# The first layer's leading products from x itself, with the tokens' factors applied to the outputs

## The chip, the cores and the metric

The kernel runs on one core of one Trainium2 chip. The metric is device time in microseconds (us) for one execution. TensorE (PE) does matrix products into PSUM banks, VectorE (DVE), ScalarE (ACT) and GpSimd (POOL) do elementwise work, SyncE (SP) issues most loads and stores. The engines run at the same time, each in its own fixed order, and wait for one another through semaphores.

## What is computed

Two layers of an encoder over 512 tokens of width 1024. Each layer begins with a normalisation and one wide projection; its output feeds a neighbourhood attention (A), a dilated attention (B) and an attention into 256 memory tokens (M), which are gated, merged and projected; then comes a gated MLP. What matters for this change:

```python
def rms_norm(x, g):
    xf = x.astype(jnp.float32)
    y = xf * lax.rsqrt(jnp.mean(xf * xf, axis=-1, keepdims=True) + RMS_EPS)
    return (y * g.astype(jnp.float32)).astype(x.dtype)

def reference(x, mem, mem_norm_g, g_pre_mix, w_in, ...):
    mem_n = rms_norm(mem, mem_norm_g)
    for l in range(DEPTH):
        h = rms_norm(x, g_pre_mix[l])
        proj = h @ w_in[l]
        q_a, k_a, v_a, q_b, k_b, v_b, q_m, gate_pre = jnp.split(proj, splits, axis=-1)
...
        o_m = memory_attention(q_m, mem_n, w_mem_kv[l])
```

The factor `rsqrt(mean(x*x) + eps)` is one number for each token. In the product `h @ w_in` it can stand in front of the sum over the 1024 channels: the gain `g` cannot, since it differs from channel to channel.

## The kernel before

**Layout.** Everything is held transposed: channels on the 128 partitions, tokens along the free dimension. x is eight tiles of 128 channels by 512 tokens (k = 0 to 7). Tokens are handled in two halves of 256 where a normalisation is waited for.

**Products in three parts.** Each float32 operand is split into a high part (a rounded copy by ACT, `split`, L220) and a low part (the difference, by DVE or POOL). `mm3` (L246) makes high x high, high x low and low x high. A weight tile is loaded by SP into a raw buffer (`wraw`, three of them), then split by `weights` (L224). With `slot` given, high and low parts go into tiles of 512 columns from a pool: two ACT casts and two differences for each weight tile.

**The leading products.** In front of each normalised stage, six output tiles are computed together in six PSUM banks (`group_banks`, L427, `run_group`, L430): in layer 0 the output tiles `FIRST` = 0, 3, 6, 1, 4, 7, that is q, k and v of two pairs of heads of A. They run as three pairs (0, 1, 2 in the text), for half 0 and then for half 1; for each k a pair takes six matmuls of 256 columns. Their inputs come from `pre_norm_job` (L347): `first_squares` (L782) squares x on ACT and adds on DVE; `rstd_job` (L323) sums over the partitions with products against a column of 1/1024, takes Sqrt on ACT and the reciprocal on DVE, multiplies the identity with the factors (two diagonal matrices, DVE), and one float32 product with a matrix of ones spreads the factors over all partitions in a PSUM bank; `normed` (L342) makes x * g * factor on DVE, the high part on ACT and the low part on DVE, for each k.

**The order.** `Woven` (L46) fixes PE's order: it keeps a clock of the PE work issued so far (`clk`), jobs with due times on that clock are put between the matmuls by `tick`, and `need` runs jobs until a flag is given. The orders of the other engines follow from a planner at build time that goes by the order of issue and by when it takes the inputs to be ready. The start of the kernel (L792 to L805) issues: x's first half, the constants (`ident`, `vec`, which holds the gains, and `mg` on POOL's queue), the squares, two weight tiles, x's second half, the normalisation of half 0, then that of half 1 four units later, the other four weight tiles, the tables, and the memory tokens' normalisation (`mem_norm_job`, L380, whose loads are on ACT's queue).

**After the leading products** the keys and values of the memory come (`mem_kv`, L408, called at L813), then the evacuations of the six banks (`a_q`, `a_k`, `a_v`), a third triple of projections (`proj`, L442), and the projections of B, between which the heads of A run as jobs.

**Pools.** `mp` holds 32 tiles of 512 columns (`big`), `hp` 16 more (`htile`) for the normalised tiles and some weights. `ytile` is a pool of 8.

Of the kernel before, what the change touches and what calls it, by code (L numbers as in the profile page):

```python
# [7 lines left out]
F32 = mybir.dt.float32  # L8
# [24 lines left out]
V_N = 232  # L33
# [86 lines left out]
def tile_hybrid_encoder(ctx, tc, xT, memT, memg, vecs, rpb, w_in, w_kv, w_bra, w_brb, w_brm,  # L120
# [6 lines left out]
    mp = ctx.enter_context(tc.tile_pool(name="mp", bufs=32))  # L127
    hp = ctx.enter_context(tc.tile_pool(name="hp", bufs=16))
# [17 lines left out]

    def htile(dt=F32R, shape=(128, 512)):
        return hp.tile(list(shape), dt, tag="h", name=nm("h"))
# [41 lines left out]
    def load_x(half):  # L190
        for k in range(0, KD, 2):
            nc.sync.dma_start(out=xs[k // 4][:, k % 4:k % 4 + 2, half], in_=xT[:, k:k + 2, half])

    load_x(HALVES[0])
# [5 lines left out]
    ones = const.tile([128, 128], F32, name="ones")  # L200
    nc.gpsimd.memset(ones, 1.0)
# [4 lines left out]
    vec = const.tile([128, depth, V_N], F32, name="vec")  # L206
    nc.gpsimd.dma_start(out=vec, in_=vecs)
# [16 lines left out]
    def weights(src, K, C, slot=None, eng=None, after=None):  # L224

        raw = wp.tile([128, K, C], F32, tag="wraw", name=nm("wraw"))
        nc.sync.dma_start(out=raw, in_=src)
# [95 lines left out]
    def rstd_job(accs, n, box):  # L323
# [11 lines left out]
        diag = small("h32", 4, (128, n))  # L335
        for b in range(nb):
            V.tensor_scalar_mul(diag[:, 128 * b:128 * b + 128], ident, rs[:, b:b + 1])
        yield 1.2
        mm(pr, ones, diag, True, True, n * 4 / 2400.0)
        box.append(pr)  # L340

    def normed(src, g, rs, hi, lo, eng=None):  # L342
        h32 = small("h32", 4)
        V.scalar_tensor_tensor(out=h32, in0=src, scalar=g, in1=rs, op0=ALU.mult, op1=ALU.mult)
        split(h32, hi, lo, eng)

# [29 lines left out]
    def h_tiles():  # L376
        return [(htile(), htile()) for _ in range(KD)]


    def mem_norm_job(l, hm, slot):  # L380
# [5 lines left out]
        acc = small("h32", 4)  # L386
# [43 lines left out]
    def run_group(grp, hs, half, flag, cols=None):  # L430
# [4 lines left out]
        for i in range(0, len(ws), 2):  # L435
            for k in range(n):
                rhs = [t[:, half] for t in hs[k]]
# [365 lines left out]
    hm = []  # L803
    wv.spawn(mem_norm_job(0, hm, big), 6.0)
    km, vm = [], []  # L805
# [205 lines left out]
```

## Time and profile before

| | us |
|---|---|
| runs before, median of 3 | 1577.96 (1577.94 to 1579.77) |
| the profiled execution | 1579.04 |
| its span, first to last instruction | 1577.3 |
| busy in the span: PE | 1529.7 |
| busy in the span: DVE | 911.2 |
| busy in the span: ACT | 727.4 |
| busy in the span: POOL | 186.4 |

A row of the order of time reads: start, time to the end of the merged instructions, engine, line of the kernel, operation, output <- inputs, shapes, count, and in brackets the idle time in front and what ended it. A helper records most operations of ACT and DVE, so they all have its line (L114); matmuls have L244. In the groups by line the columns behind the bar are busy time in us and mean duration in ns, and behind the second bar the idle time just in front. Tiles go by the program's names without numbers: `h` and `m` are pool tiles, `mm`, `s`, `o` and `pt` PSUM banks, `wraw`, `whi`, `wlo` weight tiles, `y` work tiles.

### The profile page before, as it was taken

The numbers are of one execution on the slowest core, as the hardware profiler recorded it, in microseconds if no ns is written. First come the engines' busy times: TensorE is split into PE (matmuls) and PEld (weight loads), VectorE is DVE, ScalarE is ACT, GpSimd is POOL, SyncE is SP. The second block draws the span as 40 slices with busy tenths as digits, with TensorE's granted clock in tenths as the row PEclk, the third lists the DMA queues.
The fourth block names the chain that finished last, engine by engine and source line by source line (L and its number), as shares of the span: only waits on it lengthen the run. The fifth ranks groups of instructions, "written<-read, shape, count | busy, mean of one in ns | idle before, by whom it ended". The sixth has DMA issues, their size and how long they took to land.

```text
span 1577.3 us, 21375 instructions
## 1 busy us (share of the span) xinstructions
PE 1529.7 (97%) x8246; PEld 1316.4 (83%) x8246; DVE 911.2 (58%) x1654; ACT 727.4 (46%) x1289; POOL 186.4 (12%) x244
## 2 busy tenths in 40 slices
PE   6999999999999999999989999999999999999997
PEld 5988888889898888878888888888898888888887
DVE  6686566344866666542386856743457666664233
ACT  5465575334544444532345646733454544444231
POOL 4340000110400000010062300001121000000000
PEclk9999999999999999999999999999999999999998
DMA  7222213224213222333331221132431232223331
GB/s 241 87 78 67 66 56 100 88 94 134 81 42 106 93 95 96 115 97 100 115 113 49 86 69 56 51 120 74 140 101 48 69 105 95 94 96 96 99 103 62
DMA packets 46614, 144.96 MB, mean 92 GB/s; under 512 B 5232, under 2 KB 11376, under 8 KB 46512
## 3 DMA queue, kind: packets, MB, share of 16 engines
q1 hardware_dynamic: 44656, 139.61, 27.7%
q10 hardware_dynamic: 1152, 2.10, 0.5%
q0 software_dynamic: 704, 1.88, 0.4%
q8 instruction: 65, 1.06, 0.3%
q14 instruction: 37, 0.30, 0.1%
HBM read 141.47 MB, written 2.10 MB: 91 GB/s over the span
## 4 chain that ended last, share of the span: by engine, by line
PE 88%; DVE 8%; ACT 2%; issue 1%; DMA 1%; SPq 0%; ACTq 0%
PE mm L244 73%; PE s L244 6%; PE o L244 3%; PE pt L244 2%; DVE h L114 2%; PE pt L255 2%; DVE y L114 2%; DVE x L114 1%; DVE m L114 1%; DVE wlo L114 1%; ACT whi L114 1%; DVE acc L114 1%; DVE ka L114 0%; ACT y L114 0%; DMA m<-in_memT_dram 0%
## 5 line engine op out<-in xcount | busy, mean ns | idle before, releaser
L244 PE MATMUL mm<-h,whi 128*128 128x512 f32 x2432 | 755.7, 392 | 0.0
L244 PEld LDWEIGHTS mm<-h,whi 128*128 128x128 f32 x2432 | 449.6, 188 | 88.7
L114 DVE TENSOR_TENSOR wlo<-wraw,whi 128x1024 fp32r<-128x1024 f32 (+1 forms) x203 | 246.9, 1218 | 394.9 <-ACT whi L114 394.8
L244 PE MATMUL mm<-h,wlo 128*128 128x512 f32 x1216 | 473.9, 390 | 0.0
L114 ACT CAST whi<-wraw 128x1024 fp32r<-128x1024 f32 (+1 forms) x203 | 210.3, 1038 | 296.5 <-PE mm L244 295.7
L244 PEld LDWEIGHTS mm<-h,wlo 128*128 128x128 f32 x1216 | 228.2, 188 | 48.5
L244 PE MATMUL mm<-m,whi 128*128 128x512 f32 (+1 forms) x672 | 178.2, 354 | 1.6 <-DVE m L114 0.8
L244 PEld LDWEIGHTS mm<-m,whi 128*128 128x128 f32 x672 | 119.6, 192 | 19.0 <-PE mm L244 1.3
L114 DVE SCALAR_TENSOR_TENSOR y<-mm,vec,y 128x511 f32<-128x511 f32 x160 | 118.9, 746 | 8.5 <-ACT y L114 5.9
L244 PE MATMUL mm<-m,wlo 128*128 128x512 f32 (+1 forms) x336 | 118.3, 352 | 0.7 <-DVE wlo L114 0.7
L114 ACT ACTIVATE y<-mm,vec 128x512 f32<-128x512 f32 (+1 forms) x163 | 113.6, 698 | 0.1
L244 PE MATMUL mm<-m,m 128*128 128x512 f32 (+1 forms) x432 | 88.6, 346 | 0.0
L222 POOL TENSOR_TENSOR m<-wraw,m 128x512 fp32r<-128x512 f32 x42 | 56.3, 1355 | 238.5 <-ACT m L114 234.2
L728 POOL TENSOR_TENSOR m<-m,y 128x512 f32<-128x512 f32 x28 | 36.1, 1289 | 405.7 <-DVE y L114 405.7
L244 PEld LDWEIGHTS mm<-m,m 128*128 128x128 f32 x432 | 67.6, 190 | 8.4
L244 PEld LDWEIGHTS mm<-m,wlo 128*128 128x128 f32 x336 | 64.4, 192 | 9.4 <-DVE wlo L114 1.1
L114 ACT ACTIVATE y<-y 128x512 f32<-128x512 f32 x44 | 27.8, 632 | 87.3 <-DVE y L114 87.3
L244 PE MATMUL mm<-h,m 128*128 128x256 f32 x456 | 63.6, 296 | 4.0 <-ACT h L114 1.6
L114 DVE TENSOR_TENSOR acc<-acc,sq 128x256 f32<-128x256 f32 (+1 forms) x86 | 44.6, 521 | 37.5 <-ACT sq L114 36.9
L114 ACT CAST m<-wraw 128x512 fp32r<-128x512 f32 (+1 forms) x98 | 56.1, 602 | 21.1 <-DMA wraw<-in_w_brb_dram 9.5
L244 PEld LDWEIGHTS mm<-h,m 128*128 128x128 f32 x456 | 59.2, 199 | 6.4 <-ACT h L114 2.8
L114 ACT CAST m<-pt 128x512 fp32r<-128x512 f32 (+1 forms) x72 | 38.2, 539 | 40.4 <-PE pt L255 32.0
(150 smaller groups left out, 1835.8 us busy)
## 6 DMA issues: line engine op xcount, KB each, us to landing
wraw<-in_w_in_dram SPq DMA_DIRECT2D x88, 512.0 KB, 3.3
wraw<-in_w_up_dram SPq DMA_DIRECT2D x88, 512.0 KB, 3.3
wraw<-in_w_down_dram SPq DMA_DIRECT2D x32, 512.0 KB, 3.5
wraw<-in_w_out_dram SPq DMA_DIRECT2D x16, 512.0 KB, 3.4
wraw<-in_w_down_dram SPq DMA_DIRECT2D x16, 384.0 KB, 3.1
wraw<-in_w_kv_dram SPq DMA_DIRECT2D x8, 512.0 KB, 3.6
wraw<-in_w_bra_dram SPq DMA_DIRECT2D x16, 192.0 KB, 2.3
x<-in_xT_dram SPq DMA_DIRECT2D x8, 256.0 KB, 7.2
```

What stands on the lines that cost most here:

```text
L114: return op(*args, **kw)
L222: last_lo[eng or V] = (eng or V).tensor_sub(lo, src, f32(hi)).ins
L244: wv.pe(nc.tensor.matmul(ps, a, b, start=first, stop=last), cost)
L255: wv.pe(nc.tensor.transpose(ps[:, 128 * i:128 * i + 128], s, ident), 0.11)
L728: (V if br == 2 and m >= 6 else G).tensor_add(acc[m], acc[m], gs)
```

## The change

Half 0 of the first layer's leading products no longer uses normalised tiles. `raw_split` makes the high and low part of x * g, without the token factors; the products run on these (`xg`) into columns 0 to 255 of the six banks. Half 1 runs on normalised tiles as before. A tile `R` holds the factors of half 0 (copied from PSUM) and 1.0 for half 1; after both halves every bank is multiplied by `R` into a work tile (`scaled`), and the evacuations read that tile. Half 0 is normalised all the same, later, since all other projections use it: `first_norm_job(1, R)` is due at 13 units, `first_norm_job(0, R)` at 22.

The loads of x's first half and of the first two weight tiles, cut into halves, alternate on SP's queue. The gains (`vec`) are loaded on ACT's queue ahead of everything. All weight tiles of this group have their low parts on DVE; two of them follow the split of x, then x's second half is issued, then the last two. The memory tokens' normalisation is spawned after the first pass of the products, and `mem_kv` runs after the third triple of projections.

In every `rstd_job` the diagonal matrices and the product with ones are replaced by two products of the identity with the factors' column, read 128 times by a zero step; the pause in front of them falls from 1.2 to 0.8 units. The pools `mp` and `hp` become one of 48; what used `htile` uses `big`.

```diff
-    mp = ctx.enter_context(tc.tile_pool(name="mp", bufs=32))
-    hp = ctx.enter_context(tc.tile_pool(name="hp", bufs=16))
+    mp = ctx.enter_context(tc.tile_pool(name="mp", bufs=48))
...
-    load_x(HALVES[0])
+    vec = const.tile([128, depth, V_N], F32, name="vec")
+    nc.scalar.dma_start(out=vec, in_=vecs)
...
+    def load_w(src, K, C, ks=None, raw=None):
+        if raw is None:
+            raw = wp.tile([128, K, C], F32, tag="wraw", name=nm("wraw"))
+        ks = ks or slice(0, K)
+        nc.sync.dma_start(out=raw[:, ks, :], in_=src[:, ks, :])
+        return raw
...
-        diag = small("h32", 4, (128, n))
+        yield 0.8
         for b in range(nb):
-            V.tensor_scalar_mul(diag[:, 128 * b:128 * b + 128], ident, rs[:, b:b + 1])
-        yield 1.2
-        mm(pr, ones, diag, True, True, n * 4 / 2400.0)
+            one = rs[:, b:b + 1]
+            spread = bass.AP(one.tensor, one.offset, [list(one.ap[0]), [0, 128]])
+            mm(pr[:, 128 * b:128 * b + 128], spread, ident, True, True, 0.22)
...
+    def raw_split(l, goff, k, src, hi, lo):
+
+        g = vec[:, l, goff + k:goff + k + 1]
+        ACT.activation(hi, src, AF.Copy, scale=g)
+        V.scalar_tensor_tensor(out=lo, in0=src, scalar=g, in1=f32(hi), op0=ALU.mult, op1=ALU.subtract)
...
+    def scaled(ps, R):
+        y = ytile()
+        V.tensor_mul(y, ps, R)
+        return y
...
-    hs = h_tiles()
-    wv.spawn(pre_norm_job(0, V_PRE, first_squares(HALVES[0]), hs, 0))
-    gw = group_weights([w_in[0, m] for m in FIRST[:2]], (V, G))
+    def first_norm_job(i, R):
+
+
+        half, box = HALVES[i], []
+        yield from rstd_job(first_squares(half), 256, box)
+        if i == 0:
+            ACT.copy(R[:, half], box[0])
+        for k in range(KD):
+            normed(x[k][:, half], vec[:, 0, V_PRE + k:V_PRE + k + 1], box[0], hs[k][0][:, half], hs[k][1][:, half])
+        crit[0] = last_copy[0]
+        yield 1.2
+        wv.give(f"h0.{V_PRE}.{i}")
+
+    hs, R = h_tiles(), rtile()
+    nc.gpsimd.memset(R[:, HALVES[1]], 1.0)
+    xg = [big(F32R, (128, 2, 256)) for _ in range(KD)]
+    xg = [(t[:, 0, :], t[:, 1, :]) for t in xg]
+    load_x(HALVES[0], (0,))
+    raws = [load_w(w_in[0, m], KD, 128, slice(0, 4)) for m in FIRST[:2]]
+    load_x(HALVES[0], (2,))
+    for m, raw in zip(FIRST, raws):
+        load_w(w_in[0, m], KD, 128, slice(4, 8), raw)
+    load_x(HALVES[0], (4, 6))
+    gw = []
+    for k in range(KD):
+        raw_split(0, V_PRE, k, x[k][:, HALVES[0]], *xg[k])
+        if k == 0:
+            gw += [weights(None, KD, 128, big, raw=raw) for raw in raws]
+    gw += group_weights([w_in[0, m] for m in FIRST[2:4]], (V, V))
     load_x(HALVES[1])
-    wv.need(f"h0.{V_PRE}.0")
-    with tc.issue_after(last_copy[0]):
-        sqs = first_squares(HALVES[1])
-    wv.spawn(pre_norm_job(0, V_PRE, sqs, hs, 1), SD1)
-    gw += group_weights([w_in[0, m] for m in FIRST[2:]], (V, G, V, G))
+    gw += group_weights([w_in[0, m] for m in FIRST[4:]], (V, V))
+    wv.spawn(first_norm_job(1, R), 13.0)
+    wv.spawn(first_norm_job(0, R), 22.0)
...
     for l in range(depth):
         pss = group_banks()
-        for i in range(2):
-            run_group((gw, pss), hs, HALVES[i], f"h{l}.{V_PRE}.{i}")
+        if l == 0:
+            run_group((gw, pss), xg, FULL, None, HALVES[0])
+            wv.spawn(mem_norm_job(0, hm, big), 6.0)
+            run_group((gw, pss), hs, HALVES[1], f"h0.{V_PRE}.1")
+            wv.need(f"h0.{V_PRE}.0")
+            pss = [scaled(ps, R) for ps in pss]
+        else:
+            for i in range(2):
+                run_group((gw, pss), hs, HALVES[i], f"h{l}.{V_PRE}.{i}")
         fence = crit[0]
-        if l == 0:
-            mem_kv(l, hm, km, vm)
...
+        if l == 0:
+            mem_kv(l, hm, km, vm)
```

More of the change, by code (lines that the diff above doesn't have):

```diff
@@ L222, in split, with weights @@
         last_lo[eng or V] = (eng or V).tensor_sub(lo, src, f32(hi)).ins
-    def weights(src, K, C, slot=None, eng=None, after=None):
-        raw = wp.tile([128, K, C], F32, tag="wraw", name=nm("wraw"))
-        nc.sync.dma_start(out=raw, in_=src)
+    def load_w(src, K, C, ks=None, raw=None):
[4 more added lines that the diff above has]
+        return raw
+    def weights(src, K, C, slot=None, eng=None, after=None, raw=None):
+        if raw is None:
+            raw = load_w(src, K, C)
         if slot is None:
@@ L376, in h_tiles @@
     def h_tiles():
[L377 removed]
+        return [(big(), big()) for _ in range(KD)]
     def mem_norm_job(l, hm, slot):
```

28 lines of the change are left out of this document (11 added, 17 removed).

## The prediction

> **What bounds the kernel now.** I read the busy times first, then the chain that ended last, then the busy time of stretches, and last the order of time of the first 60 us.
>
> ```profile
> span 1577.3 us, 21375 instructions
> PE 1529.7 (97%) x8246; PEld 1316.4 (83%) x8246; DVE 911.2 (58%) x1654; ACT 727.4 (46%) x1289; POOL 186.4 (12%) x244
> ...
> PE 88%; DVE 8%; ACT 2%; issue 1%; DMA 1%; SPq 0%; ACTq 0%
> ...
> 0.00:12.00 12.00, 1.84 (x8) 1.78 (x8) 2.46 (x6) 4.57 (x12) 5.98 (x35) 1.00 0.81 264
> 12.00:48.00 36.00, 31.19 (x220) 29.64 (x221) 30.44 (x64) 20.73 (x51) 15.09 (x16) 1.00 0.59 198
> 48.00:58.40 10.40, 10.40 (x89) 10.40 (x88) 7.30 (x19) 3.81 (x11) 1.73 (x3) 1.00 0.11 42
> 58.40:71.50 13.10, 12.19 (x100) 11.84 (x99) 7.17 (x10) 6.40 (x11) 7.35 (x13) 1.00 0.28 91
> 71.50:130.00 58.50, 57.16 (x311) 48.51 (x309) 48.45 (x128) 38.79 (x88) 19.56 (x25) 1.00 0.27 89
> 130.00:160.00 30.00, 29.96 (x154) 25.08 (x153) 14.58 (x31) 14.46 (x26) 1.08 (x2) 1.00 0.19 60
> ```
>
> TensorE (PE) is busy for 97% of the span, and the chain of waits runs through it for 88%, so only two things can shorten the kernel: PE work removed or PE gaps closed. The second part of the fence is busy time per stretch (start:end, length, then busy us of PE, PEld, DVE, ACT, POOL, the clock, the DMA share, GB/s). PE has nothing to do for 10 of the first 12 us. The profiled execution took 1579.04 us, its span 1577.3; the median of the three shown is 1577.96. I sum against 1579.04 and subtract the 1.1 us between it and the median at the end.
>
> ```profile
> 9.90 1.84 PE L244 MATMUL pt<-mean,y 128*128 128x1 f32 x8 [9.90 <-DVE y L114]
> 15.10 0.58 PE L244 MATMUL mm<-h,m 128*128 128x256 f32 x1 [1.01 <-ACT h L114]
> 16.65 7.65 PE L244 MATMUL mm<-h,m 128*128 128x256 f32 x41 [0.96 <-DVE h L114]
> 25.20 0.60 PE L244 MATMUL pt<-mean,y 128*128 128x1 f32 x4 [0.90 <-DVE y L114]
> ...
> 47.80 5.02 PE s L244 x42
> ...
> 58.42 0.40 PE L244 MATMUL mm<-m,whi 128*128 128x256 f32 x2
> ```
>
> In order of time: the first PE work is the sum of squares (9.90), the first leading product comes at 15.10, the last ends where the memory keys begin (58.42). The leading products are 6 banks x 2 halves x 8 x 3 = 288 matmuls of 256 columns. Run without a gap, 42 take 5.02 us in the chain of waits, 0.12 each: 288 need 34.6 us. From 0 to 58.42 PE thus loses some 20 us after the small norm products (1.84 and 0.60 among them, about 4 in all): about 15 before the first, the rest while 41 matmuls take 7.65 us because they follow the normalised tiles one by one. That stretch is what the change touches.
>
> **The change, part by part.** *The start.* Half 0 no longer waits for squares, means, Sqrt, reciprocal, diagonals and spread: it waits for a column of x, the gain vector and a weight half, then one ACT cast and one DVE instruction for each.
>
> ```profile
> 0.75 1.97 SPq L192 DMA_DIRECT2D x<-in_xT_dram  x4
> 2.77 0.94 SPq L227 DMA_DIRECT2D wraw<-in_w_in_dram  x2
> ...
> 0.00:10.00 10.00, 0.10 (x1) 0.13 (x1) 2.37 (x6) 4.35 (x10) 5.98 (x35) 1.00 0.75 241
> 10.00:20.00 10.00, 6.87 (x26) 5.79 (x27) 7.81 (x20) 5.86 (x14) 2.64 (x2) 1.00 0.88 296
> ...
> DMA to landing us min/median/max: 2.8/7.2/8.4
> DMA to landing us min/median/max: 4.8/5.8/6.6
> ...
> DMA to landing us min/median/max: 7.3/7.4/8.1
> ```
>
> First two issues on SyncE's queue, then the DMA rate of two stretches, then the landing times of x, of the memory tiles on ACT's queue, and of the first weight tiles. 241 GB/s are 2.4 MB by 10.0. In the new order x's first half (1.05 MB), two weight tiles (1.05) and the constants (0.3) are 2.4 MB, so the eighth column lands at 10 to 11 whatever the interleaving; the first lands at 0.75 + 2.8 = 3.5. The gain vector moves from POOL's queue to the head of ACT's; a load on that queue has landed after 4.8 to 6.6 us, an x load after 2.8: 3.6 to 7.4. Behind the cast that waits for it stand the weight casts in ACT's order, so PE waits for the vector too. POOL's queue only loses an issue: the identity comes no later.
>
> ```profile
> L114 DVE TENSOR_TENSOR h<-h,h 128x256 fp32r<-128x256 f32 x16 | 8.8, 565 | 1.1 <-ACT h L114 1.1
> L222 POOL TENSOR_TENSOR m<-wraw,m 128x512 fp32r<-128x512 f32 x6 | 8.0, 1356 | 17.0 <-ACT m L114 17.0
> L114 DVE SCALAR_TENSOR_TENSOR h<-x,vec,pt 128x256 f32<-128x256 f32 x16 | 7.1, 471 | 0.2 <-PE pt L244 0.2
> L114 ACT CAST m<-wraw 128x512 fp32r<-128x512 f32 x12 | 6.7, 615 | 0.0
> L114 ACT CAST h<-h 128x256 fp32r<-128x256 f32 x16 | 6.4, 402 | 4.0 <-DVE h L114 3.8
> L114 DVE TENSOR_TENSOR m<-wraw,m 128x512 fp32r<-128x512 f32 x6 | 3.9, 683 | 0.0
> ...
> L114 DVE TENSOR_TENSOR y<-y,y x6: 411/422/1536, 22.0 to 25.1; 128x256 f32<-128x256 f32 x6
> ...
> 92.15 0.69 DVE L114 TENSOR_TENSOR m<-pt,m 128x512 fp32r<-128x512 f32 x1 [0.85 <-ACT m L114]
> ```
>
> Durations (busy time over count): a 128x256 scalar-tensor-tensor 0.44 us, a 128x256 cast 0.40, a weight cast 0.56, a weight difference 0.65 on DVE and 1.36 on POOL; a 128x256 add 0.42 (the median), a 128x512 tensor-tensor from PSUM 0.69. The 128x256 differences average 0.55, but those beside no POOL work took 0.42, and after the change no weight difference runs on POOL in this stretch. The new scalar-tensor-tensor for x (cast, then 0.44) and the PSUM multiply have these rows as their nearest.
>
> PE could start between 5.5 (vector at 3.6) and 9.4 (vector at 7.4), the last 1.9 being an x cast, a weight cast, a weight difference and their hand-overs; I take 7.0. Pair 0 then follows the loads: last column at 10.5, two casts and differences and 6 matmuls, end at 13.0. Pair 1 needs the fourth weight tile, which waits for the first raw buffer and may go to the queue before or after x's second half (1.05 MB, 3.6 us at 290 GB/s): landed at 13.3 or 16.9, usable 1.2 later (0.56 + 0.65). I take 16.0; end 21.8. Pair 2's last tile is landed at 20.5 in both orders: 21.8 to 27.6, with one norm job's PE work inside (0.60 for the means in the 25.20 row, as much for the two spread products): 28.8. Half 1's first tile comes after that job's spread: 0.44 + 0.40 + 0.42, of which one k (0.72) is covered: 29.4. Its three pairs take 17.3, the first paced by DVE at 0.86 for 0.72 (+1.1), and half 0's own norm job adds 1.2: 49.0. **Lead: 58.4 - 49.0 = 9.4 us earlier.** Best case 7.0 + 34.6 + 2.4 = 44.0, so 14.4. Worst case: 2.1 more for a fourth tile usable at 18.1 and 2.9 for a wait of the same kind in front of the last tile: 54.0, so 4.4.
>
> *A cold array.* The first 15 matmuls are slower than the later ones in the same bank:
>
> ```profile
> L244 PE MATMUL mm<-h,m x15: 415/415/580, 16.6 to 19.8; 128*128 128x256 f32 x15
> ...
> L244 PE MATMUL mm<-h,m x27: 279/283/415, 19.8 to 24.0; 128*128 128x256 f32 x27
> ```
>
> 415 against 283 ns until 20 us, though the granted clock reads 1.00. Started at 7.0 at this cost, six matmuls take at most 6 x (0.12 + 0.13) = 1.5 us, so three ks pass before 11.5, when the last columns arrive anyway: I cost it at 0, and at 4.5 us if all of pair 0 stayed slow. The Trainium skill, "TensorE: Matmul & The Clock Gate", section "Part 1: The HAM clock gate", says that the array runs at half speed until it has been busy for about 3.4 us. The slow rows end 3.3 us after 16.65, which agrees. The rule speaks against a start on trickling data: an estimate by that page is half of 3.4, 1.7 us lost, and the sum would be 1571.3.
>
> *The norm job everywhere.* Two diagonal multiplies on DVE and a product with ones become two products of the factors' column spread by a zero step. 18 jobs have it; on PE it matters where PE waited for the diagonals:
>
> ```profile
> 412.88 0.67 PE L244 MATMUL pt<-h,ones 128*128 128x256 f32 x2 [1.47 <-DVE h L114]
> 787.61 0.67 PE L244 MATMUL pt<-h,ones 128*128 128x256 f32 x2 [1.27 <-DVE h L114]
> 812.65 0.67 PE L244 MATMUL pt<-h,ones 128*128 128x256 f32 x2 [3.04 <-DVE h L114]
> 1188.61 1.19 PE L244 MATMUL pt<-h,ones 128*128 128x256 f32 x2 [0.89 <-DVE h L114]
> 1567.70 0.48 DVE L114 TENSOR_SCALAR h<-ident,st 128x128 f32<-128x128 f32 x2
> 1568.34 0.99 PE L244 MATMUL pt<-h,ones 128*128 128x256 f32 x2 [1.16 <-DVE h L114]
> ```
>
> The chain loses 0.48 of DVE and about 0.15 of handover, 0.63 us. The yield falls from 1.2 to 0.8, so the product also stands 0.4 earlier in PE's order with less cover. Five waits then give 0.23 to 0.63 each: 1.2 to 3.2; I take 2.0, and 0 as the low end (the next wait, on the cast, ends last). The zero-step weight load is in no row; the nearest is the ones pair, 0.67: no gain or loss there, half a microsecond either way.
>
> *Multiplying the outputs.* A projection of the third triple, from the chain of waits:
>
> ```profile
> 85.53 5.46 PE mm L244 x24
> ```
>
> Six 0.69 multiplies, 4.1 us of DVE, four of them beside half 1's last products, the last two behind it. The next PE work, the third triple of projections, has a free third bank and needs half 0's normalised tiles, which DVE makes meanwhile (8 x 0.86 = 6.9). On DVE the evacuations and that triple's weight differences stand behind the multiplies, which themselves wait for ACT's copy of the factors, one of 0.4. This triple (3 x 5.46 = 16.4 us of PE) now covers the six evacuations that the 13.1 us of memory keys covered. I cost it at 0 on PE; without that cover it is the 1.4 us of the last two.
>
> *Memory keys later; DVE.* PE does the same 13 us of key work, so the move is free unless DVE cannot follow. DVE was busy 95.8 us up to 130 (the first five stretches). Added: three weight tiles taken from POOL, 6 x 0.65 = 3.9; x's differences 8 x 0.44 = 3.5; multiplies 4.1; removed three diagonal pairs, 1.4: 105.9. The same point should now come at 120.6 (130 - 9.4), with DVE idle for the first 6: 92% full. From 71.5 to 130 it was at 48.45 of 58.50, 83%, from 12 to 48 at 85%, neither at its limit. At 90% it needs 105.9/0.90 + 6 = 123.7. I take that, +3.1; bounds 0 (130 to 160 has DVE only half busy, and a lag there need not reach PE) and the gap at 83%, 133.6 - 120.6 = 13.0.
>
> *One pool of 48* in place of 32 and 16: the tiles are the same number, and in the first stretch 16 + 8 + 24 are exactly 48, so the memory tiles, four issues on ACT's queue, wait until the eight x tiles come free at about 29; they land some 6 us later, well ahead of the third triple. Later stages keep their order of requests: 0, up to 2 either way.
>
> Sum: -9.4 - 2.0 + 3.1 = -8.3: 1570.7 beside 1579.04, or **1569.6** on the median's footing.
>
> **The rivals.** (1) *All of the lead is kept:* loads arrive without gaps and DVE follows: 14.4 + 2 - 1.5 = 15 less, 1563. For it: the loads need only 20 of the 44 us. Against it: pair 1 waits for a tile that waits for a buffer. (2) *DVE becomes the bound behind the lead.* If it fills to 83% only, PE reaches the old 130 mark at 133.6: 3.6 later, less 2.0 elsewhere: 1579.5. (3) **Slower:** the same place at 80% or less: 105.9/0.80 + 6 = 138.4, 8.4 later, 2 back: 1584. It decides from about 82%, where the waits behind DVE stand in PE's fixed order (heads' transposes) and the other projections cannot pass them. For it: 58.40 to 71.50 and 71.50 to 130.00 already left PE idle for 0.9 and 1.3 us. Against it: less POOL work in the way of DVE's differences, and DVE's light stretch behind. (4) *The early start does not come:* the gain vector is last (7.4) and the fourth tile stands behind the second half of x and the tables: lead 4.4, norm jobs 2.0, given back 3.1: 1574.6, at the edge of what can be told apart, and counted there as no change.
>
> **How the numbers follow.** Forecast 0.58; rival 1 0.14; rival 2 0.12; rival 3 0.10; rival 4 0.06. 0.2% is 3.2 us, about what a measurement of this kernel can tell from no change: the bound lies at 1574.8 and 1581.2. Faster: forecast and rival 1, 0.72; within: rivals 2 and 4, 0.18; slower: 0.10. The range leaves out rival 3 and the better half of rival 1: 1562 to 1580.
>
> **What would show it.** The first leading product at 6 to 9 us instead of 15.10; the first projection with whi tiles (no key work before it) at 47 to 52; pair 1 starting when its second tile lands; DVE above 88% between 10 and 115 with PE waits on DVE below 5 us there; the listed norm waits each shorter by half a microsecond. The prediction is wrong if the start is later than 10, if PE waits more than 10 us behind DVE between 49 and 120, or if a stage after 160 changes by more than 3 us.

## The result, and the profile after

| | us |
|---|---|
| before, median of 4 runs | 1578.63 (1577.94 to 1579.77) |
| after, median of 4 runs | 1598.33 (1597.16 to 1599.57) |
| ratio | 1.0119, interval 1.0102 to 1.0136 |
| predicted | 1569.6, range 1562 to 1580 |

The change makes the kernel 20 us slower; it was forecast to be 9 us faster. Below are, of the kernel after, the busy times, the shares of the chain that ended last, and busy time by stretch in the same stretches and columns as in the prediction.

```profile
span 1597.8 us, 21397 instructions
PE 1537.3 (96%) x8282; PEld 1325.2 (83%) x8282; DVE 902.3 (56%) x1638; ACT 733.3 (46%) x1298; POOL 180.8 (11%) x237
...
PE 84%; DVE 8%; issue 4%; ACT 2%; DMA 1%; POOL 0%; SPq 0%; ACTq 0%; POOLq 0%; DVEq 0%
```

```profile
0.00:12.00 12.00, 3.59 (x10) 2.49 (x11) 4.21 (x9) 6.30 (x13) 5.73 (x34) 1.00 0.81 273
12.00:48.00 36.00, 35.41 (x279) 35.01 (x279) 23.42 (x59) 18.78 (x50) 0.00 (x0) 1.00 0.48 170
48.00:58.40 10.40, 3.93 (x29) 3.29 (x27) 10.27 (x21) 8.21 (x15) 4.11 (x6) 0.78 0.04 13
58.40:71.50 13.10, 8.10 (x29) 6.57 (x30) 6.54 (x7) 0.86 (x2) 9.07 (x10) 0.65 0.26 90
71.50:130.00 58.50, 52.37 (x310) 46.34 (x309) 47.54 (x123) 36.30 (x83) 21.71 (x31) 0.94 0.27 82
130.00:160.00 30.00, 30.00 (x169) 25.79 (x169) 21.32 (x53) 17.32 (x37) 3.52 (x7) 1.00 0.24 83
```

From 12 to 48 PE is fuller than before (35.4 of 36 us, against 31.2): the early start works. From 48 to 71.5 PE is busy for 12.0 of 23.5 us where it was busy for 22.6, and the granted clock reads 0.78 and 0.65 where it read 1.00. The DVE column names the stretch in front of it: 10.27 of 10.40 us. From 130 to 160 DVE is busy for 21.3 us where it was busy for 14.6, but PE is full there.

The order of time on PE, rows with a wait, and one row where the second pair of banks begins:

```profile
5.98 1.30 PE L244 MATMUL mm<-m,m 128*128 128x256 f32 x3 [5.98 <-ACT m L114]
9.50 1.60 PE L244 MATMUL mm<-m,m 128*128 128x256 f32 x4 [2.22 <-ACT m L114]
...
18.47 5.92 PE L244 MATMUL s<-m,m 128*128 128x256 f32 x48
...
31.77 0.38 PE L244 MATMUL mm<-m,m 128*128 128x256 f32 x1 [0.29 <-ACT m L114]
...
52.67 0.73 PE L244 MATMUL mm<-m,whi 128*128 128x512 f32 x2 [1.47 <-ACT whi L114]
63.40 0.79 PE L244 MATMUL mm<-m,wlo 128*128 128x512 f32 x1 [10.00 <-DVE wlo L114]
81.64 1.09 PE L255 MATMUL pt<-ident,sq 128*128 128x128 f32 x4 [4.22 <-DVE h L114]
104.22 0.44 PE L255 MATMUL s<-ident,m 128*128 128x128 f32 x2 [1.91 <-ACT m L114]
```

The lead ends at 51.2 (52.67 less the wait of 1.47), 7.2 us earlier than the 58.42 of before. Then the third triple of projections starts at once, and after its first two products it waits 10.0 us for the low part of its weights. What DVE does meanwhile:

```profile
53.45 0.68 DVE L114 TENSOR_TENSOR y<-pt,R 128x512 f32<-128x512 f32 x1
54.14 1.39 DVE L114 TENSOR_TENSOR m<-y,m 64x512 fp32r<-64x512 f32 x2
55.54 1.70 DVE L114 SCALAR_TENSOR_TENSOR ka<-y,ka 64x512 fp32r<-64x512 f32 x2
57.27 0.59 DVE L114 COPY sq<-y 128x64 f32<-128x64 f32 x2
57.90 2.16 DVE L114 TENSOR_TENSOR m<-y,m 64x512 fp32r<-64x512 f32 x2
60.09 1.71 DVE L114 SCALAR_TENSOR_TENSOR ka<-y,ka 64x512 fp32r<-64x512 f32 x2
61.82 3.07 DVE L114 TENSOR_TENSOR wlo<-wraw,whi 128x1024 fp32r<-128x1024 f32 x2
```

The last multiply of a bank by the factors ends at 54.1, then come the evacuations of six banks (54.1 to 61.8), and only then the two weight differences that PE waits for. DVE is never idle; PE waits for the last thing in its line. The four waits behind the lead sum to 17.6 us, where the kernel before had two of 2.1 together:

```profile
65.18 0.47 PE L244 MATMUL mm<-m,whi 128*128 128x256 f32 x2 [0.84 <-DVE m L114]
81.20 0.63 PE L255 MATMUL pt<-ident,sq 128*128 128x128 f32 x4 [1.28 <-DVE sq L114]
```

The other 5 us of this part's loss are matmuls at half rate beside the waits. In the kernel after, the granted clock reads 0.50 from 53.8 to 67.4, from 81.1 to 84.5 and from 105.0 to 108.4 us; PE is busy for 4.0, 2.9 and 3.4 us of these stretches, 10.3 in all, and half of that is lost (last section). The kernel before has no such stretch there.

The loss by places, as the start of the same instruction after, less its start before (for the end of the lead the start of what follows it, less the wait; in the last row the spread of the last factors):

| up to | before | after | later by | in this part |
|---|---|---|---|---|
| end of the lead | 58.42 | 51.20 | -7.2 | -7.2 |
| attention B, first scores | 177.39 | 190.88 | 13.5 | +20.7 |
| down-projection | 671.55 | 686.73 | 15.2 | +1.7 |
| layer 1, first value transposes | 856.38 | 877.45 | 21.1 | +5.9 |
| last spread | 1568.34 | 1588.05 | 19.7 | -1.4 |

So there are two losses: 20.7 us behind the lead, and 5.9 us in the transition to layer 1. The first four experiments undo one part of the change each or mend one place, the next ones put parts together or alone into the kernel before, and the rest ask why the lead's 7.2 us don't arrive.

### The profile page after: what moved, and what is told of

Same layout as the page of the kernel before. It is cut to its first block, busy times and chain, and to the rows that moved or that the text cites. A ratio compares the mean times of both kernels' runs of the same rounds, so it can differ in the third digit from the quotient of the medians.

```text
span 1597.8 us, 21397 instructions
## 1 busy us (share of the span) xinstructions
PE 1537.3 (96%) x8282; PEld 1325.2 (83%) x8282; DVE 902.3 (56%) x1638; ACT 733.3 (46%) x1298; POOL 180.8 (11%) x237
## 4 chain that ended last, share of the span: by engine, by line
PE 84%; DVE 8%; issue 4%; ACT 2%; DMA 1%; POOL 0%; SPq 0%; ACTq 0%; POOLq 0%; DVEq 0%
PE mm L244 72%; PE s L244 5%; PE o L244 3%; DVE m L114 2%; PE pt L244 2%; PE pt L255 2%; DVE y L114 2%; DVE x L114 1%; DVE h L114 1%; DVE wlo L114 1%; DVE acc L114 1%; DMA wraw<-in_w_in_dram 1%; DVE ka L114 1%; ACT m L114 1%; ACT y L114 1%
## 5 line engine op out<-in xcount | busy, mean ns | idle before, releaser
L244 PE MATMUL mm<-m,whi 128*128 128x512 f32 (+1 forms) x3104 | 935.0, 384 | 2.1 <-ACT whi L114 2.1
L244 PEld LDWEIGHTS mm<-m,whi 128*128 128x128 f32 x3104 | 569.7, 189 | 108.7 <-ACT whi L114 2.7
L244 PE MATMUL mm<-m,wlo 128*128 128x512 f32 (+1 forms) x1552 | 593.0, 382 | 10.7 <-DVE wlo L114 10.7
L244 PEld LDWEIGHTS mm<-m,wlo 128*128 128x128 f32 x1552 | 293.0, 189 | 68.4 <-DVE wlo L114 11.6
L244 PE MATMUL mm<-m,m 128*128 128x256 f32 (+1 forms) x1008 | 170.7, 320 | 13.9 <-ACT m L114 8.8
L244 PEld LDWEIGHTS mm<-m,m 128*128 128x128 f32 x1008 | 144.0, 198 | 25.1 <-ACT m L114 9.5
L244 PE MATMUL s<-m,m 128*128 128x256 f32 (+2 forms) x672 | 93.5, 294 | 6.1 <-DVE m L114 4.0
L244 PEld LDWEIGHTS s<-m,m 128*128 128x128 f32 x672 | 88.1, 197 | 10.6 <-DVE st L114 4.2
L244 PE MATMUL o<-m,m 128*128 128x256 f32 (+2 forms) x448 | 75.8, 294 | 1.2 <-DVE m L114 1.2
L244 PEld LDWEIGHTS o<-m,m 128*128 128x128 f32 (+1 forms) x448 | 60.2, 172 | 7.8 <-issue 2.5
```

Of the source, the lines that this page charges most:

```text
L244: wv.pe(nc.tensor.matmul(ps, a, b, start=first, stop=last), cost)
```

## The experiments

Each is compared with the kernel before on the same chip, whose median was 1578.5 to 1580.0.

**Third triple's weights first.** The changed kernel with this edit (`proj` takes the tiles made ahead):

```diff
+            ahead = [weights(w_in[l, 3 * i + 2], KD, 128) for i in range(2)]
             pss = [scaled(ps, R) for ps in pss]
```

> The changed kernel, with the first two weight tiles of the third triple split ahead of the six multiplies and evacuations, and without the order behind half 0's last cast. Theory A (order): PE waited 10.0 us at 63.40 because DVE's fixed order had the six multiplies and the twelve evacuation instructions in front of the first low part. Then that wait falls below 2 us, the half-rate matmuls behind it go with it, and the time falls by 10 to 13 us, to about 1586. Theory B (DVE has too much work up to 130 us): the work is the same, so the wait turns up at the heads' transposes and the time falls by less than 4 us, to 1594 or more.

Measured: 1590.58, ratio 1.0069 (1.0052 to 1.0086). 7.7 us better, between the two theories. The wait of 10.0 becomes one of 3.0, but a new one of 4.7 us stands at 63.2, where memory's factors now wait on DVE. A backlog: whatever is moved forward, the next thing is late.

**Memory keys first**, as they were:

```diff
         fence = crit[0]
+        if l == 0:
+            mem_kv(l, hm, km, vm)
```

> The changed kernel, with the memory keys back in front of the evacuations. Theory A (order): the keys do not cure the order by themselves, since their weights' low parts and the memory's normalised tiles stand behind the normalisation of half 0 and beside the multiplies on DVE; a wait of 5 to 15 us stays, now in front of the keys, and the waits of 4.2 us (the value transposes, behind the memory's normalisation) and 1.9 us go: 1592 to 1602. Rival (the later keys are the loss): the wait of 10 us goes as well, 13 of the 20 us come back: 1585 or less.

Measured: 1586.72, ratio 1.0044 (1.0029 to 1.006). 11.6 us come back, a little less than the rival's 13, and attention B begins at 179.24 instead of 190.88:

```profile
55.51 1.22 PE L244 MATMUL pt<-ident,st 128*128 128x128 f32 x4 [2.47 <-DVE st L114]
58.05 1.26 PE L244 MATMUL mm<-m,whi 128*128 128x256 f32 x2 [1.32 <-ACT m L114]
...
179.24 0.71 PE L244 MATMUL s<-m,m 128*128 128x128 f32 x4 [0.46 <-DVE st L114]
```

The waits of 10.0, 4.2 and 1.9, which theory A expected to stay in part, are gone; one of 2.5 us for memory's factors and one of 1.3 on its casts remain. The move of the keys is the largest single loss: they are 13 us of PE work, and of the evacuations only two instructions on DVE (1.7 us) stand in front of the memory's tiles.

**Two pools**, 32 and 16, as they were:

```diff
-    mp = ctx.enter_context(tc.tile_pool(name="mp", bufs=48))
+    mp = ctx.enter_context(tc.tile_pool(name="mp", bufs=32))
+    hp = ctx.enter_context(tc.tile_pool(name="hp", bufs=16))
```

> The changed kernel with the two pools of 32 and 16 tiles again, and the h tiles where they were. Theory P (the one pool delays tiles at the layers' transitions): the 5.9 us lost between 680 and 877 us and the 1.7 us lost between 213 and 687 come back: 1590 to 1592. Rival N (the shortened norm job reorders the engines there): no change within 2 us: 1597 to 1599. The first 130 us do not change under either.

Measured: 1592.17, ratio 1.0083 (1.0064 to 1.0102): 6.2 us better. The transition's loss falls from 5.9 to 1.1, about as theory P said; another 2.1 come in the first 130 us, where both theories expected nothing. In the kernel after, these rows of ACT and PE show what the single pool did:

```profile
819.50 0.40 ACT L114 CAST m<-h 128x256 fp32r<-128x256 f32 x1 [0.48 <-DVE h L114]
820.39 0.41 ACT L114 CAST m<-h 128x256 fp32r<-128x256 f32 x1 [0.48 <-DVE h L114]
821.11 0.41 ACT L114 CAST m<-h 128x256 fp32r<-128x256 f32 x1 [0.32 <-DVE h L114]
821.54 0.37 ACT L114 COPY m<-mm 128x256 f32<-128x256 f32 x1
```

```profile
821.97 0.69 PE L255 MATMUL s<-ident,m 128*128 128x128 f32 x2 [3.30 <-ACT m L114]
836.14 4.18 PE L244 MATMUL s<-m,m 128*128 128x256 f32 x18 [4.03 <-DVE m L114]
```

The copy of memory's values out of PSUM stands behind all eight casts of the next layer's tiles, and PE's transposes of it wait 3.3 us. In the kernel before, the same copy stood behind the first of these casts (at 803.02). The number of tiles is the same. I take it that their order of release, and with it the order that the planner gives ACT, is not; the run shows that the pool brings this wait about, not by which tile.

**Old norm job** in the changed kernel (diagonals, a product with ones, pause 1.2; a block of `R` that holds 1.0 serves for the ones):

```diff
-        yield 0.8
+            V.tensor_scalar_mul(diag[:, 128 * b:128 * b + 128], ident, rs[:, b:b + 1])
+        yield 1.2
+        mm(pr, ones, diag, True, True, n * 4 / 2400.0)
```

> The changed kernel with the old norm job: diagonal matrices, product with ones, pause of 1.2. Theory N (the shorter pause and the earlier spread put the memory values' copies behind the eight casts of h on ACT): the 5.9 us at the layers' transition come back, against some 3 us lost at the norm waits that the spread had shortened: 1593 to 1598. Theory P (the pool): the transition stays as slow and the norm waits come back on top: 1599 to 1602.

Measured: 1597.3, ratio 1.0112 (1.0097 to 1.0127): 1.0 us better, which is within the noise. By the trace, 3.2 of the transition's 5.9 come back and 1.7 are lost up to attention B. The second wait of the fence above, 4.03, falls to 1.24: with the new job the residual's adds start earlier (828.2 instead of 832.2), and they stand on DVE in front of the low part of memory's values that frees PE's bank `s`. That low part ends at 836.0 or 836.1 in both runs; what comes back is above all that the 45 matmuls behind the shorter wait take 5.62 us and not 8.32.

**Keys first and two pools together**, both edits above:

> The changed kernel with the memory keys and values back in front of the evacuations and the two pools (32 and 16) back; the lead's new form and the norm job stay. Theory A, the two losses stand in different places (hand-over at 50 to 85 us, transition between the layers at 810 to 840) and add up: 1598.3 - 11.6 - 6.2 = 1580.5, within 1.5. Rival B, they overlap, since the two pools alone already gave 2.1 of their 6.2 in the first 130 us, where the keys give theirs: 1582.5 to 1584. Both expect the 3.3 us wait on ACT's value copy near 820 to be gone.

Measured: 1580.65, ratio 1.0005 (0.9995 to 1.0014). The sum of the two single runs is 1580.5: they add up, as theory A said.

**Norm job alone** in the kernel before:

```diff
-            V.tensor_scalar_mul(diag[:, 128 * b:128 * b + 128], ident, rs[:, b:b + 1])
-        yield 1.2
-        mm(pr, ones, diag, True, True, n * 4 / 2400.0)
+        yield 0.8
...
+            mm(pr[:, 128 * b:128 * b + 128], spread, ident, True, True, 0.22)
```

> The kernel before with the new norm job alone (factors' column read with a zero step, pause 0.8). The prediction's term: 2.0 us faster, 1576.5 beside 1578.5, the five waits in front of the spread products shorter by half a microsecond each. Rival, from the run of the changed kernel with the old norm job, where the layer transition was 3.2 us better and the first part 1.7 worse: about 1 us slower, with a new wait on DVE behind the spread in the transition (835 in the changed kernel).

Measured: 1577.13, ratio 0.9979 (0.9969 to 0.9989), 2.5 us faster. Attention B begins 2.2 us earlier, so nearly all of the gain is in the first stage, not spread over the kernel; in the transition a wait of 3.9 us takes the place of those of 3.0 and 0.8.

**One pool alone** in the kernel before:

```diff
-    mp = ctx.enter_context(tc.tile_pool(name="mp", bufs=32))
-    hp = ctx.enter_context(tc.tile_pool(name="hp", bufs=16))
+    mp = ctx.enter_context(tc.tile_pool(name="mp", bufs=48))
```

> The kernel before with one pool of 48 in place of 32 and 16, nothing else. The prediction's term: 0, up to 2 either way, 1576.5 to 1580.5. Rival, from the run of the changed kernel with two pools: tiles are handed out in the order in which they come free, so memory's values and the next layer's tiles get others and wait for others; 3 to 5 us slower, all of it between 672 and 870 us, with memory's value copy on ACT behind the eight casts of the next layer's tiles.

Measured: 1583.82, ratio 1.0024 (1.0015 to 1.0033), 4.2 us slower: 2.2 up to attention B, 3.9 more up to layer 1, a little back behind it. The transition's wait is that of the kernel after:

```profile
811.08 0.69 PE L254 MATMUL s<-ident,m 128*128 128x128 f32 x2 [3.38 <-ACT m L114]
```

**Norm job alone, old pause**, against the run of the norm job alone:

```diff
-        yield 0.8
+        yield 1.2
```

> The kernel before with the factors' column spread by the zero step, as in the run of the norm job alone, but with the old pause of 1.2 units in front of the spread. Theory A, the shorter diagonal chain is the gain and the shorter pause is a loss of its own, since it puts the spread products in front of other matmuls that were ready (the 3.9 us wait on DVE in the transition, 830 to 835, that the kernel before has at 0.8): that wait falls to under 1.5 and the kernel is 2 to 3 us faster than the norm job alone, 1574 to 1575.5. Rival B, the pause only moves waits about: within 1 us of the norm job alone, 1576 to 1578.

Measured: 1581.63, ratio 1.0007 (0.9997 to 1.0016), 4.5 us slower than with 0.8: both theories miss. The trace says why. ACT, then DVE, of this kernel in order of time:

```profile
35.12 0.42 ACT L114 ACTIVATE h<-m 128x256 f32<-128x256 f32 x1 [5.67 <-DMA m<-in_memT_dram]
```

```profile
28.55 0.86 DVE L114 SCALAR_TENSOR_TENSOR h<-x,vec,pt 128x256 f32<-128x256 f32 x2
35.88 0.43 DVE L114 TENSOR_TENSOR h<-h,sq 128x256 f32<-128x256 f32 x1 [6.47 <-ACT sq L114]
```

With the other pause the first add of memory's squares stands on DVE ahead of six of half 1's tiles. ACT's squares wait for memory's load until 35.1, so DVE stands still for 6.5 us, and PE waits six times for half 1's tiles. This run does not measure the shorter chain; it measures how much a change of 0.4 units can do to an order.

**Keys, pools and pause 1.2**: the same edit of the pause on the run of keys and pools together.

> The changed kernel with keys first, two pools, and a pause of 1.2 units in front of the spread products. Theory A, the 5.3 us wait on DVE in the transition of that kernel belongs to the pause: it falls to under 2 and the kernel gains 3 to 4 us on the one with a pause of 0.8, 1576.5 to 1577.5. Rival B, it belongs to the start of the kernel through another order of the tiles: the wait stays, 1580 to 1581.

Measured: 1579.84, ratio 1.0 (0.9991 to 1.0009). The transition's wait is 4.3 where it was 5.3: theory A falls here. The new job makes this wait with either pause: alone in the kernel before it is 3.9 us with a pause of 0.8 and 4.6 with 1.2, and 0.8 with the old job.

**Half 0's low parts on POOL** (on top of keys and pools; later also on top of the run told next):

```diff
-            normed(x[k][:, half], vec[:, 0, V_PRE + k:V_PRE + k + 1], box[0], hs[k][0][:, half], hs[k][1][:, half])
+            normed(x[k][:, half], vec[:, 0, V_PRE + k:V_PRE + k + 1], box[0], hs[k][0][:, half], hs[k][1][:, half], G if i == 0 else None)
```

> As the kernel with keys first and two pools, and half 0's eight low parts in the first layer made by POOL, which has nothing to do from 7 to 50 us, and not by DVE. Theory A, DVE's order is what is left of the loss behind the lead (it works without idle time from 42 to 64 us, and the 2.5 us wait for the memory's factors ends on it): 8 x 0.38 = 3.0 us of DVE less in front of that reciprocal, the waits of 2.5 and 1.3 us shrink to under 1.5 together, 2 to 4 us better than that kernel, some 1577 to 1578. Rival B, PE only waits for the next thing, or POOL's own reads slow DVE down by as much: within 1 us of that kernel.

> As the run with the memory first, with half 0's eight low parts made by POOL and not by DVE (3.0 us less on DVE between 52 and 61). Nothing is left out. Theory A, DVE's backlog is the bound and POOL has room (5.0 of 14 us busy): the wait of 4.0 falls to about 1, the B stage at 174 to 175, 2 to 3 us better than the run with the memory first. Rival B, as in the earlier run with these low parts on POOL: the third triple of projections or the evacuations' copies now wait for POOL; no gain, or up to 3 us slower.

Measured: 1583.97 (1.0025, 1.0015 to 1.0035) and 1578.31 (0.9995, 0.9986 to 1.0004). Theory A fails both times. The first is 3.3 us slower than its base, more than its rival B allowed, though the spans of the two profiled executions differ by 0.1, so its cause stays open; the second stands to the kernel before as its base does (0.9995 and 0.9996), as its rival B said, and its wait stays at 4.0.

**Memory first.** On top of keys, pools and pause: memory's normalisation is due earlier and has a shorter pause, half 0's tiles are made later and from `R`, the multiplies come ahead of both:

```diff
             ACT.copy(R[:, half], box[0])
+            wv.give("R")
+            yield 6.0
+            box = [R[:, half]]
...
-        yield 14.0
+        yield 14.0 if l else 8.0
...
-            wv.spawn(mem_norm_job(0, hm, big), 6.0)
+            wv.spawn(mem_norm_job(0, hm, big), 2.0)
...
-            wv.need(f"h0.{V_PRE}.0")
+            wv.need("R")
             pss = [scaled(ps, R) for ps in pss]
...
             mem_kv(l, hm, km, vm)
+            wv.need(f"h0.{V_PRE}.0")
```

> As the run with keys first, two pools and a pause of 1.2, and the order on DVE behind the lead changed: the memory tokens' normalisation comes ahead of half 0's, half 0's tiles are normalised from the tile of factors in SBUF while the memory keys run, and the multiplies stand ahead of both. Nothing is added or left out. Theory A, the lead's 7.3 us are lost since the memory's tiles are normalised last of four jobs on DVE (42 to 64 us) while PE waits and then runs at half rate: the memory keys now begin within 1.5 us of the lead's end and run at full rate, 5 to 7 us better than the run with keys, pools and pause, some 1570 to 1572, faster than both kernels. Rival B, DVE has more work than the stretch holds whatever the order (23 us of time, some 25 of work): the wait moves to the third triple of projections, less than 2 us better.

Measured: 1579.25, ratio 0.9996 (0.9988 to 1.0005). The keys begin without a wait, but 4.0 us are lost within their third projection, for the low part of its weights. Rival B in its result; its reason (too much work in any order) was put to the next runs.

**The same with 6.6 us of DVE's work left out** (first edit below, and half 0's low parts not made: their tiles hold zeros), and **half 0's tiles one by one**, each due 1.2 units after the last, with all the work (second edit):

```diff
-            pss = [scaled(ps, R) for ps in pss]
```

```diff
-            yield 6.0
+            yield 12.0
...
         for k in range(KD):
+            if i == 0:
+                yield 1.2
```

> As the run with the memory first, with 6.6 us of DVE's work behind the lead left out: the six multiplies of the outputs by the factors (the evacuations read the banks themselves) and half 0's eight low parts (their tiles hold zeros, written by POOL before). Theory A, DVE is full there (13.66 of 14 us between 51 and 65) and the 4.0 us wait on the memory weights' low part at 58 to 62 is its backlog: the wait falls to under 1, the matmuls behind it run at full rate, the B stage begins 4 to 6 us earlier (171 to 173 instead of 177.1), 1574 to 1575.5. Rival B, the order or the clock sets it: the wait appears in another place and the B stage begins within 1.5 us of 177.1.

> As the run with the memory first, with half 0's eight tiles due one by one (each 1.2 units of PE's work after the one before) while the memory keys run, and not all at once ahead of them. Nothing is added or left out. Theory A, the order on DVE and ACT is the cause: the keys' weights and evacuations no longer stand behind eight tiles, the wait of 4.0 us between the keys falls under 1, PE stays at full rate from 52 to 75, the B stage begins at 172 to 174 instead of 177.1, 1574.5 to 1576.5. Rival B, DVE has too much work there in any order: the wait moves to the third triple (its weights' low parts now stand behind half 0's tiles and the evacuations), the B stage within 1.5 us of 177.1, 1578 to 1580.

Measured: 1582.0 (1.002, 1.0011 to 1.0028) and 1586.38 (1.0051, 1.0035 to 1.0066). With less work the wait only moves, as rival B said, and the time doesn't fall: 3.97 us at 64.5 for the third key's bank, whose evacuation stands on DVE behind half 0's tiles. With the tiles one by one the keys run without a gap and the wait comes behind them, at the third triple, where rival B expected it; but the run is slower than either forecast. Busy time by stretch and the wait on PE, tiles one by one:

```profile
51.00:65.00 14.00, 14.00 (x118) 13.94 (x117) 13.87 (x31) 9.88 (x22) 7.14 (x10) 1.00 0.17 53
65.00:75.00 10.00, 2.77 (x20) 2.13 (x19) 9.78 (x19) 6.10 (x14) 5.45 (x8) 0.88 0.16 60
```

```profile
76.47 0.80 PE L248 MATMUL mm<-h,wlo 128*128 128x512 f32 x1 [7.36 <-DVE wlo L114]
```

PE 14.0 of 14.0 us, then 2.8 of 10, with DVE full in both. The pause of 0.8 again in place of 1.2, in this kernel:

> As the run with half 0's tiles one by one, with the pause of 0.8 units in front of the spread products instead of 1.2. In the kernel before, 0.8 and 1.2 differed by 4.5 us (1577.1 and 1581.6), all of it in the first 60 us, where half 1's tiles came later. Theory A, that gain belongs to half 1's tiles coming one by one behind the spread, and half 1 here waits for its tiles too (0.8 and 1.1 us): 0 to 2 us better. Rival B, the gain belongs to the old start only: within 1 us, as between the two runs with keys first and two pools (1580.7 and 1579.8).

Measured: 1587.27, ratio 1.0056 (1.0044 to 1.0068): rival B, no change.

**One by one with the work left out, and one by one with the third triple's weights ahead of the evacuations:**

```diff
             mem_kv(l, hm, km, vm)
+            ahead = [weights(w_in[l, 3 * i + 2], KD, 128) for i in range(2)]
             wv.need(f"h0.{V_PRE}.0")
```

> The run with half 0's tiles one by one, with the same 6.6 us of DVE's work left out as before (the six multiplies of the outputs, half 0's eight low parts). Theory A, DVE's amount of work between 42 and 78 is the bound once the order is right: the wait of 7.4 us in front of the third triple falls by about 6.6, to 1 or 2, the matmuls behind it run at full rate, the B stage begins at 174 to 178 instead of 185.0, 1574 to 1578. Rival B, something else holds the third triple (the weights' own place in the order, ACT's casts): the wait stays above 4 and the B stage begins after 181.

> The run with half 0's tiles one by one, with the third triple's first two weight tiles split ahead of the evacuations. Nothing is left out. Theory A (amount of work): the wait of 7.4 us shrinks by the 3.5 us of the four evacuations passed, and half of that comes back where the heads wait for these: 2 to 4 us better, 1582 to 1584.5. Rival B (place in the order): the wait goes, and with it the lead's gain arrives: 1576 to 1579.

Measured: 1578.48 (0.9986, 0.9976 to 0.9995) and 1577.85 (0.9985, 0.9976 to 0.9995). Taking work away removes the wait of 7.4 (theory A); so does putting the two differences in front of the evacuations, with no work taken away (rival B). In the latter:

```profile
51.00:65.00 14.00, 13.81 (x115) 13.54 (x113) 13.87 (x27) 10.08 (x22) 8.87 (x11) 1.00 0.22 76
65.00:75.00 10.00, 8.85 (x40) 7.38 (x41) 9.78 (x17) 6.38 (x12) 4.66 (x7) 1.00 0.37 120
75.00:90.00 15.00, 12.45 (x56) 10.10 (x55) 12.38 (x30) 8.50 (x20) 7.71 (x10) 0.89 0.24 79
```

This is the changed kernel's start with nothing left out, and faster than both kernels: 2.1 us below the before of its own runs. But its memory keys begin at 52.80 where they began at 58.42, and attention B at 176.64 where it began at 177.39: of 5.6 us, 0.8 arrive. DVE is full to 75, and behind it PE is busy for 12.45 of 15 us, with this wait for one of DVE's copies:

```profile
80.38 0.99 PE L259 MATMUL pt<-ident,sq 128*128 128x128 f32 x4 [2.43 <-DVE sq L114]
```

The norm job alone, without the new start, gave as much (2.5). From the first memory key to attention B it is 119.0 us before, 123.8 in this run, 120.7 in the run with the work left out (whose lead ends late, 56.35) and 130.2 with the tiles one by one alone.

## Why the prediction was wrong

**Start and lead: -9.4 predicted, -7.2 measured.** The mechanism held: the first product came at 5.98 (7.0 predicted). The size missed on the step *A cold array*, costed at 0 with 4.5 as the bound. By the groups by line, up to 20 us:

```profile
L244 PE MATMUL mm<-m,m 128*128 128x256 f32 x48 | 10.2, 381 | 8.4 <-ACT m L114 8.2 <-DVE m L114 0.2
...
L244 PE MATMUL s<-m,m 128*128 128x256 f32 x13 | 1.7, 283 | 0.0
```

The first 48 matmuls averaged 381 ns where the next took 283. The slow ones ahead of 11.3 us were hidden by waits for loads. From 11.31 to 16.80 nothing hid them: 27 matmuls took 5.5 us where 27 x 0.12 = 3.2 were due, 2.2 us lost, and not 0. I had let the arrival of the last columns hide the slow matmuls; they landed, and the slow matmuls went on. The fourth weight tile was ready at 16.0, as forecast, but pair 1 began at 18.5, and everything behind it stood 2.2 late. The prediction's other estimate, 1.7, was nearer than the 0 that I took.

My reading of the kernel before was wrong here too. The second of the two rows under *A cold array*, with a maximum of 415 ns, hides 12 more slow matmuls: in that trace they start 0.21 us apart up to 22.15, and 0.12 apart from 22.35. So the slow stretch behind 16.65 lasted 5.5 us and not 3.3, and the agreement that I read there is not in the trace; and the 41 matmuls took 7.65 us not "because they follow the normalised tiles one by one" but because 26 of them ran at half rate, without a gap. The kernel before lost some 2.4 us to its cold array, and the earlier start saves none of that.

**Norm job: -2.0 predicted, -2.5 alone.** The number held by luck: I spread it over five waits, and it came in the first stage, and only with the pause of 0.8; with 1.2 the same job is no gain (1.0007). In the changed kernel its part can't be told from 0.

**Memory keys and DVE: +3.1 predicted; this is the step that failed, with *Multiplying the outputs* (0 on PE).** For the multiplies I wrote that the third triple "now covers the six evacuations that the 13.1 us of memory keys covered", and in the same paragraph that "on DVE the evacuations and that triple's weight differences stand behind the multiplies". Put in order, the second sentence refutes the first: on DVE the differences came behind the evacuations (61.8 and 54.1 us), and a triple whose own weights stand behind the evacuations cannot cover them. The keys could, since they ran in between and needed only their own weights and the memory's tiles. The keys' move, which I called "free unless DVE cannot follow", is worth 11.6 us of the 20.7 behind the lead. And I weighed DVE by its mean up to 130 us (92%), where the wait is decided in 20 us in which it has no pause at all. Rival 3 had the right engine and the right fixed orders, but its 8.4 us came from that same mean. Two of the signs named for a wrong prediction came: PE waited 14.2 us behind DVE between 49 and 120, and a stage after 160 changed by 5.9.

**One pool: 0, up to 2, predicted; 4.2 alone, 6.2 in the changed kernel.** I had counted tiles. That "later stages keep their order of requests" did not keep the copy of memory's values ahead of the eight casts; that the tiles come free in another order is the likely reason, not a shown one.

**The sum.** Keys first takes 11.6 of the 19.7 us, two pools 6.2, together 17.7. What is left is within 0.05% of before: lead and norm job, which I had at 11.4 faster, bring about nothing without further changes; no run has the new start with the old norm job in that kernel, so the two are not told apart. The last run shows that mending DVE's order recovers 2 to 3 us (from 1.0005, or 1.0 with this run's pause, to 0.9985). For the rest, the stretch from the first key to attention B is 4.9 us longer in it than before. PE's work there is the same, 116 to 117 us at full rate in both; PE stands still for 5.5 us instead of 2.7, and it works for 3.4 us at a granted clock of 0.50 (81.5 to 84.9), which costs 1.7. The longest wait, the 2.43 us at 80.38, is for a copy that DVE makes at 80.0, behind a stretch without a pause from 62 to 78.7. With 6.6 us of DVE's work left out the stretch is 1.7 longer than before, all of it waits (4.4 us), none of it at half clock. This fits too much work on DVE (multiplies, half 0's tiles a second time), but does not show it: the light run's lead ended 3.5 us later, so DVE had that much longer to catch up, and that run was no faster in all.

## What to carry to other kernels

When an engine that stands idle early is to start earlier, list in order what its partner does at the hand-over behind it, and ask for each operand of the next PE work what stands in front of it in that order; a mean of busy time over 100 us hides a full stretch of 20. Work whose operands are ready (here the memory keys) is cover, and moving it has a price of its own. Where a build-time planner sets the orders, a merged pool or another pause is not neutral: time each part alone.

## What the runs showed that was not expected

A long wait costs more than its length. Order of time on PE in the kernel after, behind the wait of 10.0 us:

```profile
63.99 1.05 PE L244 MATMUL mm<-m,whi 128*128 128x512 f32 x2
...
66.55 1.04 PE L244 MATMUL mm<-m,whi 128*128 128x512 f32 x2
...
67.67 0.62 PE L244 MATMUL mm<-m,whi 128*128 128x512 f32 x2
```

Two matmuls took 1.05 us until 67.4 and 0.62 from there: 4.0 us at half rate, about 2 us lost, and the granted clock reads 0.50 up to 67.4. The Trainium skill, "TensorE: Matmul & The Clock Gate", section "Part 1: The HAM clock gate", says that the array falls back to half speed after an idle window of about 3.4 us and needs as long a busy one to leave it. The 4.0 us behind the 10.0 us wait agree roughly with the second figure. The first doesn't hold here, and the measurement decides: the wait of 1.91 us that ends at 104.22 is followed by half clock from 105.0 to 108.4, and the 2.43 us at 80.38 of the last run by half clock from 81.5 to 84.9, though no wait of 3.4 us stands in front of either. Each of these waits of some 2 us thus cost another 1.7 us.

At the start of the kernel the slow matmuls lasted longer than one such window, from 5.98 to about 16 (27 of them start between 11.31 and 16.80, 0.20 us apart in the mean, and 0.12 from there), with a pause of 2.2 us among them, and there the granted clock reads 1.00: the clock column alone does not show them. The clock's record in this trace begins only at 16.25 us, and at 22.32 in the kernel before, just where the matmuls become fast.
